# The sample tokens' RWKV matrices: groups of 32 tokens in 32-column and 32x32 tiles, in place of masked 128x128 matrices

## The chip, the cores and the metric

The kernel runs on one core of a Trainium2 chip. The metric is device microseconds of one execution, from which a median is taken; smaller is better. The engines are TensorE (PE in the profile, with its weight loads as PEld), VectorE (DVE), ScalarE (ACT), GpSimd (POOL) and SyncE (SP), whose queue issues most of the transfers. Each works through its own list of instructions in order and waits on semaphores of the others.

## The reference

One layer of a hybrid encoder is computed for two groups of tokens: one prompt of 256 tokens, and 8 samples of 16 tokens each, which continue from a cached state. The layer has an RWKV-7 branch, a sparse-attention branch, a gated mix of both, and an expert layer (PEER). The change touches only the samples' part of the RWKV branch. Its recurrence, per head with a 64x64 state S:

```python
def _rwkv7_step(S, inp):
    r, w, k, v, a, b = inp
    sa = jnp.einsum('bhij,bhj->bhi', S, a)
    S = S * w[:, :, None, :] + sa[..., None] * b[:, :, None, :] + v[..., None] * k[:, :, None, :]
    y = jnp.einsum('bhij,bhj->bhi', S, r)
    return S, y
...
    S_fin, ys = lax.scan(_rwkv7_step, S0.astype(f32), xs)
```

There are 16 heads. Tokens of different samples never meet in it: the 8 samples are 8 independent scans of 16 steps.

## The kernel before

The scans are not run step by step. For a stretch of tokens the recurrence is written with small triangular matrices: one that couples the tokens' a and b vectors (MB), one that couples a or r with k (MK), and the inverse of a unit triangular matrix (T). For the prompt the stretch is 64 tokens, for a sample its 16 tokens.

Heads are handled in pairs, eight of them, by `rwkv_pair`; a pair's 128 columns are two heads of 64. The 128 sample tokens of all 8 samples stand together on the 128 partitions. For each pair `rwkv_pair` makes, for MB and for MK and for each head, the 128x256 product of b (or k) with the two rows a and r of all 128 sample tokens, one fp32 matmul with 64 rows of contraction, 128 columns of weights and 256 moving columns, into a PSUM tile `fx` (two buffers), and VectorE multiplies it with the mask `ms` into `MBs` or `MKs`. The mask keeps the 16x16 blocks on the diagonal and zeroes the rest. Four such matmuls stand in each pair.

`rwkv_inverse` writes the a-b half of `MBs` to DRAM (`As`), reads the 16x16 blocks back with one block on a partition (`NL`), inverts 48 blocks at once on VectorE by 15 steps of forward substitution (the prompt's blocks are among them), writes the result to a DRAM matrix (`Bs`, zeroed once, two in turn), and reads that back as a 128x128 matrix per head, `TTs`.

`chain_s` uses them: W = A0 + MK v, U = T W, y = A0' + MB U + MK' v, each with 128x128 weights and 64 moving columns per head: two matmuls for W, two for U, four for y, in fp32. A0 and A0' are added by a matmul with the identity. W and U pass through VectorE copies from PSUM to SBUF, y through a ScalarE copy.

All matmuls of these helpers go through `mm` (line 226), so that most of PE's rows in the profile have that line; tile names tell them apart. `tp` is the place in the array, and operands of 64 or 32 rows or columns occupy a part of the array only.

The stage in which the pairs run also holds dense projections (`mm` tiles, weights split in a high and a low float32r half), the attention of the samples and the prompt (`dx`, `cKT`, `cV` tiles) and the modulation (`w_ada`). The string `ORDER` says in which order the pieces are issued; the framework's scheduler, which works from a simulated timeline, then places their instructions on the engines, so that pieces are interleaved and a changed instruction can move others. The tile pools set how far each can run ahead. Later stages (mix, expert scores, expert sums) are untouched by the change.

## Time and profile before

| | |
|---|---|
| median of 3 runs | 1801.76 us (1797.88 to 1802.8) |
| the profiled execution | 1796.01 us, span 1794.1 us |
| PE busy | 1714.5 us, 96% of the span, 12576 matmul records |
| DVE busy | 1362.0 us, 76% |
| ACT, POOL busy | 703.2 us, 700.5 us |
| the stage of the pairs | about 140 to 720 us of the span |

The span runs from the first to the last instruction; the profiled execution's own time is 1.9 us longer. In rows of the timeline the columns are start, duration, engine, line, operation, output<-inputs, rows*columns of the weights in the array, shape of the output and how many equal instructions were merged. The duration of a matmul includes its way through the array, which the next one overlaps: what a matmul costs PE is read from the starts of those that follow it. An fp32 matmul is recorded as two matmuls (two passes over the moving columns): `bx<-W,TTs` has 32 records for 16 matmuls.

### The profile page before, as it was taken

The page shows a single profiled execution, that of the slowest core. Times are in us where ns is not written, and L with a number is a line of the kernel's source. Part 1 is how long each engine was busy: PE and PEld are TensorE (multiplying, and loading weights), DVE is VectorE, ACT ScalarE, POOL GpSimd, SP SyncE. Part 2 cuts the span into 40 slices and gives each one's busy share as a digit, 9 for nine tenths or more (in the row PEclk, how much of TensorE's full clock was granted, in tenths as well). Part 3 has the DMA queues.
Part 4 walks back from the last instruction along what each step waited for, and adds up shares of the span by engine and source line. Part 5 has one row for each costly group of instructions (what it writes and reads, how often), then busy time and mean ns, then how long its engine had stood idle before and what let it go on. Part 6 is the DMA issues. An engine that isn't in the chain of part 4 may idle for free.

```text
span 1794.1 us, 33542 instructions
## 1 busy us (share of the span) xinstructions
PE 1714.5 (96%) x12576; PEld 1420.0 (79%) x12576; DVE 1362.0 (76%) x2945; ACT 703.2 (39%) x1411; POOL 700.5 (39%) x752
## 2 busy tenths in 40 slices
PE   6999899999999999999999989999999999999998
PEld 4987687777878877898888889999967667776656
DVE  3448777777867765445999999899958778887885
ACT  4533343333333333324222264488843333333232
POOL 2432242323423320024054446533356565555641
PEclk7999899999999999999999999999999999999999
DMA  8543652463365364665499989964579999999995
GB/s 298 161 128 96 198 178 63 155 195 97 101 198 158 85 217 151 219 202 166 151 336 333 347 305 370 376 228 164 201 267 373 364 377 379 364 395 345 376 378 182
DMA packets 181082, 434.11 MB, mean 242 GB/s; under 512 B 39348, under 2 KB 78388, under 8 KB 180920
## 3 DMA queue, kind: packets, MB, share of 16 engines
q1 hardware_dynamic: 144056, 297.73, 49.4%
q0 software_dynamic: 36864, 134.23, 20.1%
q8 instruction: 99, 1.62, 0.4%
q14 instruction: 63, 0.52, 0.1%
HBM read 401.65 MB, written 30.24 MB: 241 GB/s over the span
## 4 chain that ended last, share of the span: by engine, by line
PE 67%; DVE 15%; DMA 10%; issue 3%; ACT 2%; POOL 2%; SPq 0%; DVEq 0%; ACTq 0%; POOLq 0%
PE mm L226 24%; PE fx L226 15%; PE dx L226 12%; PE cp L226 8%; PE bx L226 7%; DVE raw L1570 2%; DMA w<-in_pv 2%; DVE wl L234 2%; DVE acc L1580 1%; DMA w<-in_w_ada 1%; DMA raw<-in_pv,pe 1%; DMA w<-in_w_in 1%; DMA w<-in_puT 1%; ACT wh L230 1%; DVE psi L1297 1%
## 5 line engine op out<-in xcount | busy, mean ns | idle before, releaser
L234 DVE TENSOR_TENSOR wl<-w,wh 128x1024 fp32r<-128x1024 f32 (+1 forms) x274 | 343.6, 1259 | 119.6 <-ACT wh L230 58.6
L230 ACT ACTIVATE wh<-w 128x1024 fp32r<-128x1024 f32 (+1 forms) x282 | 295.9, 1054 | 207.5 <-PE mm L226 83.0
L1559 POOL DMA_INDIRECT raw<-in_pu,pe x128 | 154.6, 1208 | 181.1 <-PE dx L226 56.0
L226 PE MATMUL fx<-h2h,wh 128*128 128x256 f32 x736 | 216.1, 294 | 7.5 <-ACT wh L230 4.5
L1559 POOL DMA_INDIRECT raw<-in_pv,pe x128 | 173.0, 1351 | 120.4 <-PE dx L226 44.9
L226 PE MATMUL fx<-h2h,wl 128*128 128x256 f32 x736 | 212.2, 289 | 7.7 <-DVE wl L234 7.4
L226 PE MATMUL fx<-h2l,wh 128*128 128x256 f32 x736 | 209.9, 285 | 0.0
L1580 DVE SCALAR_TENSOR_TENSOR acc<-raw,dots,acc 128x1024 f32<-128x1024 f32 x127 | 165.2, 1301 | 10.3 <-DMA raw<-in_pv,pe 9.1
L1570 DVE SCALAR_TENSOR_TENSOR raw<-raw,sh 128x1024 f32<-128x1024 f32 x128 | 161.8, 1274 | 12.5 <-DMA raw<-in_pu,pe 11.7
L226 PEld LDWEIGHTS fx<-h2h,wh 128*128 128x128 f32 x736 | 140.9, 191 | 12.3 <-ACT wh L230 5.9
L226 PEld LDWEIGHTS fx<-h2h,wl 128*128 128x128 f32 x736 | 140.2, 191 | 10.7 <-DVE wl L234 10.1
L226 PEld LDWEIGHTS fx<-h2l,wh 128*128 128x128 f32 x736 | 141.2, 192 | 2.2 <-issue 1.7
L226 PE MATMUL fx<-h2f,w 128*128 128x256 f32 x576 | 129.9, 387 | 6.0 <-ACT G L1471 3.1
L226 PEld LDWEIGHTS fx<-h2f,w 128*128 128x128 f32 x576 | 111.0, 194 | 23.2 <-ACT G L1471 4.0
L226 PE MATMUL mm<-LTh,wh 128*128 128x384 f32 (+2 forms) x352 | 125.1, 356 | 3.3 <-ACT wh L230 2.7
L226 PE MATMUL mm<-LTh,wl 128*128 128x384 f32 (+2 forms) x352 | 123.3, 350 | 0.6 <-DVE wl L234 0.6
L226 PE MATMUL mm<-LTl,wh 128*128 128x384 f32 (+2 forms) x352 | 122.8, 349 | 0.0
L226 PE MATMUL mm<-wh,LTh 128*128 128x256 f32 x336 | 97.9, 292 | 2.7 <-ACT qx L879 2.7
L226 PE MATMUL mm<-wh,LTl 128*128 128x256 f32 x336 | 97.6, 290 | 0.0
L226 PE MATMUL mm<-wl,LTh 128*128 128x256 f32 x336 | 97.3, 290 | 0.0
L1393 POOL TENSOR_TENSOR G<-G,wg 128x144 f32<-128x144 f32 (+1 forms) x64 | 55.5, 889 | 95.6 <-ACT wg L1390 95.6
L1471 ACT ACTIVATE G<-fx 128x256 f32<-128x256 f32 x76 | 28.8, 383 | 122.8 <-PE fx L226 116.6
(560 smaller groups left out, 4193.2 us busy)
## 6 DMA issues: line engine op xcount, KB each, us to landing
w<-in_puT SPq DMA_DIRECT2D x128, 512.0 KB
w<-in_pv SPq DMA_DIRECT2D x128, 512.0 KB
w<-in_w_in SPq DMA_DIRECT2D x70, 512.0 KB
w<-in_w_ada SPq DMA_DIRECT2D x48, 512.0 KB
cKT<-in_cKT SPq DMA_DIRECT2D x32, 256.0 KB
cV<-in_cV SPq DMA_DIRECT2D x32, 256.0 KB
w<-in_w_pq SPq DMA_DIRECT2D x16, 512.0 KB
d<-wst SPq DMA_DIRECT2D x8, 832.0 KB
```

Source lines behind the costliest of these rows:

```text
L226: return self.nc.tensor.matmul(out, l, r, start=start, stop=stop, skip_group_check=True, **kw)
L230: self.nc.scalar.activation(hi, src, AF.Copy)
L234: (self.nc.vector if eng == "v" else self.nc.gpsimd).tensor_tensor(lo, src, hi, op=OP.subtract)
L1297: nc.vector.max_index(si[:, half, h, 8:16], sv[:, half, h, 8:16], s2)
L1393: (nc.vector if w is p else nc.gpsimd).tensor_tensor(g, g, w[:, :, c0:c1], op=OP.mult)
L1471: nc.scalar.activation(g, p, AF.Gelu_apprx_tanh)
L1559: d = nc.gpsimd.indirect_dma_start(out=u, out_offset=None, in_=src, in_offset=bass.IndirectOffsetOnAxis(ap=e[:, j:j + 1], axis=0))
L1570: nc.vector.scalar_tensor_tensor(u, u, 1.0, h2, op0=OP.mult, op1=OP.mult, accum_out=dots[:, j:j + 1])
L1580: nc.vector.scalar_tensor_tensor(acc, v, dots[:, j:j + 1], acc, op0=OP.mult, op1=OP.add)
```

## The change

`ms` is folded to 32 columns per half: row p of the mask speaks of the 32 tokens of p's group. For MB and MK, each head's product is made in four matmuls, one for each group of 32 tokens (two samples), with 32 weight columns and 64 moving columns (32 of a, 32 of r), each into its own 32 PSUM partitions; the PSUM tile has 64 columns instead of 256, and so have `MBs`, `MKs` and VectorE's multiplications. `As` and `Bs` hold 32x32 blocks; each is written or read by one DMA for each head, two where one stood. `TTs` has 32 columns per head. In `chain_s` each matmul with `MK`, `TT` or `MB` becomes four with 32x32 weights on the array's diagonal, and for y the MK part is issued ahead of the MB part.

```diff
-    same = (p[:, None] // 16) == (p[None] // 16)
-    c["ms"] = np.concatenate([same & (p[:, None] < p[None]), same & (p[:, None] <= p[None])], 1).astype(np.float32)
+    q = p[:, None] // 32 * 32 + np.arange(32)[None]
+    same = (p[:, None] // 16) == (q // 16)
+    c["ms"] = np.concatenate([same & (p[:, None] < q), same & (p[:, None] <= q)], 1).astype(np.float32)
...
+G32 = [slice(g, g + 32) for g in range(0, 128, 32)]
...
-            b = self.dt_([64, 516])
-            nc.sync.dma_start(b, z[:64, :516])
+            b = self.dt_([66, 128])
+            nc.sync.dma_start(b, z[:66, :128])
...
-            m_s = self.t([128, 2, 256], tag=tg + "s", bufs=2)
+            m_s = self.t([128, 2, 64], tag=tg + "s", bufs=2)
...
-            p = [self.ps([128, 256], tag="fx") for _ in prs]
+            p = [self.ps([128, 64], tag="fx") for _ in prs]
             for par, pr in enumerate(prs):
-                self.mm(p[par], src[pr, 0:128], ARs[pr].rearrange("p a l -> p (a l)"), tp=(64 * par, 0))
+                for gr in G32:
+                    self.mm(p[par][gr].rearrange("p (a l) -> p a l", a=2), src[pr, gr], ARs[pr, :, gr], tp=(64 * par, gr.start))
...
-        nc.sync.dma_start(sub_ap(As, 0, [[128, 128], [16512, 2], [1, 128]]), MBs[:, :, 0:128])
+        bs = lambda t, par: sub_ap(t, 4224 * par, [[1056, 4], [32, 32], [1, 32]])
+        for par in range(2):
+            nc.sync.dma_start(bs(As, par), MBs[:, par, 0:32])
...
-        ls = lambda t: sub_ap(t, 0, [[2064, 16], [128, 16], [1, 16]])
+        ls = lambda t: sub_ap(t, 0, [[528, 16], [32, 16], [1, 16]])
...
-        TTs = self.t([128, 2, 128], tag="TTs")
-        nc.sync.dma_start(TTs, sub_ap(Bs, 0, [[128, 128], [16512, 2], [1, 128]]))
+        TTs = self.t([128, 2, 32], tag="TTs")
+        for par in range(2):
+            nc.sync.dma_start(TTs[:, par], bs(Bs, par))
...
         for h in range(2):
-            self.mm(pw[:, hs(h)], MK[:, h, 0:128], vi[:, hs(h)], start=False, stop=True)
+            for gr in G32:
+                self.mm(pw[gr, hs(h)], MK[gr, h, 0:32], vi[gr, hs(h)], start=False, stop=True, tp=(gr.start, gr.start))
...
         for h in range(2):
-            self.mm(pu[:, hs(h)], TT[:, h], W[:, hs(h)])
+            for gr in G32:
+                self.mm(pu[gr, hs(h)], TT[gr, h], W[gr, hs(h)], tp=(gr.start, gr.start))
...
         for h in range(2):
-            self.mm(py[:, hs(h)], MB[:, h, 128:256], U[:, hs(h)], start=False, stop=False)
-            self.mm(py[:, hs(h)], MK[:, h, 128:256], vi[:, hs(h)], start=False, stop=True)
+            for gr in G32:
+                self.mm(py[gr, hs(h)], MK[gr, h, 32:64], vi[gr, hs(h)], start=False, stop=False, tp=(gr.start, gr.start))
+        for h in range(2):
+            for gr in G32:
+                self.mm(py[gr, hs(h)], MB[gr, h, 32:64], U[gr, hs(h)], start=False, stop=True, tp=(gr.start, gr.start))
```

Three places of PE's list, before and after. In the names, `mm` tiles are dense projections, `A` is A0, and the number behind a tile's name is its buffer. An `x4` in these lists counts matmuls as the program has them. First the product of b with a and r for one head of the first pair, before:

```order
L226 MATMUL mm_2485<-wl_2456,LTh_168 128x256
L226 MATMUL fx_1396<-ARs_1371,kk_1339 128x256
L226 MATMUL mm_2485<-wh_2455,LTl_169 128x256
L226 MATMUL mm_2485<-wh_2455,LTh_168 128x256
L226 MATMUL mm_2485<-wl_2456,LTh_168 128x256
```

The same place after the change:

```order
L230 MATMUL mm_2561<-wh_2531,LTl_169 128x256
L230 MATMUL mm_2561<-wh_2531,LTh_168 128x256
L230 MATMUL fx_1396<-ARs_1371,kk_1339 32x64 x4
L230 MATMUL fx_1407<-ARp_1372,kk_1339 64x128 x4
L230 MATMUL mm_2561<-wl_2532,LTh_168 128x256
```

One matmul has become four, and the prompt's products (`ARp`) now follow at once. Second, W of the first pair in `chain_s`, before:

```order
L226 MATMUL mm_4365<-wh_4361,LTh_168 128x256
L226 MATMUL bx_1695<-cfirst,A_314_1674 128x128
L226 MATMUL bx_1695<-vn_1445,MKs_1413 128x64 x2
L226 MATMUL dx_2991<-kT_2444,qTp_2443 128x128 x2
L226 LDWEIGHTS idb
```

and after:

```order
L230 MATMUL bx_1709<-cfirst,A_314_1688 128x128
L230 MATMUL bx_1709<-vn_1457,MKs_1419 32x64 x6
L230 MATMUL cp_1659<-Sb_1582,NX_1609 64x64 x2
L230 MATMUL bx_1709<-vn_1457,MKs_1419 32x64 x2
L230 MATMUL dx_3067<-kT_2520,qTp_2519 128x128 x2
```

The eight matmuls with 32x32 weights are parted by two of the prompt's chain with 64x64 weights. Third, y of the first pair, before:

```order
L226 MATMUL bx_1704<-cfirst,A_314_1674 128x128
L226 MATMUL bx_1704<-U_1694,MBs_1393 128x64
L226 MATMUL bx_1704<-vn_1445,MKs_1413 128x64
L226 MATMUL bx_1704<-U_1694,MBs_1393 128x64
L226 MATMUL bx_1704<-vn_1445,MKs_1413 128x64
L226 MATMUL dx_3012<-vv_2445,set_3016 128x64 x2
```

and after:

```order
L230 MATMUL bx_1730<-cfirst,A_314_1688 128x128
L230 MATMUL bx_1730<-vn_1457,MKs_1419 32x64 x8
L230 MATMUL bx_1730<-U_1708,MBs_1393 32x64 x8
L230 MATMUL dx_3088<-vv_2521,set_3099 128x64 x2
L230 MATMUL mm_4569<-wh_4507,LTl_169 128x256
```

Four matmuls have become sixteen, with the ones with MK ahead of those with MB.

## The prediction

> **What bounds the kernel now.** I read the page first: the busy time of each engine and the chain that ended last.

> ```profile
> span 1794.1 us, 33542 instructions
> PE 1714.5 (96%) x12576; PEld 1420.0 (79%) x12576; DVE 1362.0 (76%) x2945; ACT 703.2 (39%) x1411; POOL 700.5 (39%) x752
> PE 67%; DVE 15%; DMA 10%; issue 3%; ACT 2%; POOL 2%; SPq 0%; DVEq 0%; ACTq 0%; POOLq 0%
> ```

> Two thirds of the chain are PE's. The pairs all lie in one stage, so I asked for the busy time of that stage alone, and for what PE waited for in it (us in total, times, longest).

> ```profile
> core 0: us, PE busy (x) PEld busy (x) DVE busy (x) ACT busy (x) POOL busy (x), PEclk, DMA share, GB/s
> 140.00:720.00 580.00, 563.45 (x6065) 459.78 (x6064) 427.30 (x1162) 203.94 (x495) 173.17 (x254) 0.98 0.48 147
> PE dx L948 <- DVE qr L872: 3.6, 2, 3.0
> PE mm L226 <- ACT qx L879: 2.7, 2, 1.6
> ```

> PE is idle for 580.00 − 563.45 = 16.6 us, in small pieces. DVE is busy for 427 of 580 and ACT for 204. So PE's work sets the end of this stage, and what follows it starts when it ends: a microsecond off PE here is nearly a microsecond off the end.

> **What the change touches on PE.** Per pair there are four products with `ARs` and eight matmuls in `chain_s`. Their price is what they push the dense matmuls apart. First a product with `ARs`, in the timeline of PE (a product is one matmul, two passes, x2):

> ```profile
> 159.47 0.28 PE L226 MATMUL mm<-wl,LTh 128*128 128x256 f32 x1
> 159.68 0.70 PE L226 MATMUL fx<-ARs,kk 64*128 64x256 f32 x2
> 160.31 0.39 PE L226 MATMUL mm<-wh,LTl 128*128 128x256 f32 x1
> 160.53 0.28 PE L226 MATMUL mm<-wh,LTh 128*128 128x256 f32 x1
> ```

> From the dense start ahead of it to the second one behind it are 1.06 us. Two dense steps of 0.12 would stand there anyway (the rows 272.63 and 272.75 below are such a step), so the visit costs 0.82.

> Then two visits of 64x64 tiles, with 4 and with 16 passes of 64 moving columns:

> ```profile
> 271.93 0.28 PE L226 MATMUL mm<-wh,LTl 128*128 128x256 f32 x1
> 272.14 0.33 PE L226 MATMUL cp<-Sb,NX 64*64 64x64 f32 x4
> 272.40 0.39 PE L226 MATMUL mm<-wh,LTh 128*128 128x256 f32 x1
> 272.63 0.28 PE L226 MATMUL mm<-wl,LTh 128*128 128x256 f32 x1
> 272.75 0.28 PE L226 MATMUL mm<-wh,LTl 128*128 128x256 f32 x1
> ```

> ```profile
> 243.31 0.34 PE L226 MATMUL mm<-LTl,wh 128*128 128x384 f32 x1
> 243.58 0.68 PE L226 MATMUL cp<-TN,NO 64*64 64x64 f32 x16
> 244.19 0.44 PE L226 MATMUL mm<-LTh,wl 128*128 128x384 f32 x1
> 244.47 0.34 PE L226 MATMUL mm<-LTh,wh 128*128 128x384 f32 x1
> 244.64 0.34 PE L226 MATMUL mm<-LTl,wh 128*128 128x384 f32 x1
> ```

> The first costs 0.70 − 0.24 = 0.46, the second 1.16 − 0.35 = 0.81 (the step there is 0.17 to 0.175). Twelve passes more cost 0.35: 0.029 a pass. What is left of the first, 0.46 − 4 × 0.029 = 0.34, is the price of going to another tile shape and back, 0.17 a switch. So the `ARs` product is 0.34 of switches and 0.48 of passes, 0.24 for 256 columns or 0.06 for 64.

> U of `chain_s` uses the whole array, as the dense matmuls do, and pays no switch:

> ```profile
> 530.55 0.34 PE L226 MATMUL mm<-LTh,wh 128*128 128x384 f32 x1
> 530.73 0.55 PE L226 MATMUL bx<-W,TTs 128*128 128x64 f32 x4
> 531.09 0.42 PE L226 MATMUL mm<-LTl,wh 128*128 128x384 f32 x1
> 531.34 0.34 PE L226 MATMUL mm<-LTh,wl 128*128 128x384 f32 x1
> ```

> It costs 0.79 − 0.35 = 0.44 for four passes, 0.11 each, though only 64 columns move: that is nearer to loading 128 columns of weights than to moving 64. W has the same form. The eight passes of y, from the first to what follows them:

> ```profile
> 277.80 0.33 PE L226 MATMUL bx<-U,MBs 128*128 128x64 f32 x2
> ...
> 278.64 0.61 PE L226 MATMUL dx<-vv,set 128*128 128x64 f32 x4
> ```

> 0.84. So `chain_s` has 2 × 0.44 + 0.84 = 1.72 us of such passes in a pair.

> **Part by part.** Removed on PE: 32 `ARs` products (8 pairs × 4) × 0.48 = 15.4 us of passes, and 8 × 1.72 = 13.8 us in `chain_s`: 29.1 us together.

> Added: 128 matmuls for the `ARs` products, 256 passes, and 8 × 32 = 256 matmuls in `chain_s`, 512 passes: 768 passes of 64 moving columns on tiles of 32 columns. No row has such a tile with so few columns. The two nearest prices are the two-abreast 0.029 above (two 64x64 tiles on the diagonal) and this place, where a `cp` and a `bx` group use all four 64x64 tiles:

> ```profile
> 262.20 0.22 PE L226 MATMUL cp<-MBp,cQ 64*64 64x64 f32 x1
> 262.21 0.22 PE L226 MATMUL bx<-cQ,bn 64*64 64x64 f32 x1
> 262.21 0.22 PE L226 MATMUL cp<-MBp,cQ 64*64 64x64 f32 x1
> 262.21 0.22 PE L226 MATMUL bx<-cQ,bn 64*64 64x64 f32 x1
> 262.26 0.22 PE L226 MATMUL cp<-MBp,cQ 64*64 64x64 f32 x1
> ...
> 262.27 0.22 PE L226 MATMUL cp<-MBp,cQ 64*64 64x64 f32 x1
> ```

> Four passes start within 0.01 us, the next four 0.06 us later: 0.015 a pass with four tiles at work. The new groups have four tiles each (four diagonal ones, or four column groups of one row half), so I take 0.015: 768 × 0.015 = 11.5 us. With 0.029 it would be 22.3.

> Switches: I counted in both programs' lists how often PE's tile shape changes from one matmul to the next: 556 times before, 603 after. The `ARs` products only change one partial shape for another; `chain_s`, which paid nothing, now goes to 32x32 and back 26 times, and some groups are parted, as W of the first pair is. 47 × 0.17 = 8.0 us.

> Sum on PE: 11.5 + 8.0 − 29.1 = −9.6 us; with 0.029 a pass, +1.2. Below −9.6 there is room only if both heads' products run together on eight tiles, at half the price for 256 passes: −1.9 more. The order keeps most of them apart.

> Not on the path: VectorE's 32 mask multiplications.

> ```profile
> L605 DVE TENSOR_TENSOR MBs<-fx,cfront x16: 394/421/425, 157.0 to 613.1; 128x256 f32<-128x256 f32 x16
> L672 SPq DMA_DIRECT2D d<-MBs x8: 359/374/378, 160.9 to 613.6; - x8
> SPq L672 <- DVE MBs L605: 20.3, 4, 8.2
> ```

> At 0.42 us and a quarter of the columns they can save at most 32 × 0.42 = 13 us of DVE's 427, where DVE is not the bound: nothing, covered by PE; were that cover gone, a gain and no loss. The DMAs move a quarter of the bytes in as many pieces, each a quarter as long, and one more write and one more read is issued per pair: 16 × 0.37 = 6 us of SP's queue over the stage. The write waits for MBs (20.3 us in 4 waits), with the weight loads behind it in the queue; now two writes wait, the first for one head and the second for both, so the last of them goes no later than the one before did. I price this at nothing, with the loads ahead in four buffers as cover; if that fails, the loss is of the size of the issue, 6 us at most.

> How much reaches the end: between the chain's PE share, 0.67, and all. I take 0.8, since PE's idle pieces in the stage are few: −7.7 us. The rearranged order can add to or take from the 16.6 us that PE idles; I allow 5 us either way, about a third of it.

> The sum is against the profiled execution, 1796.0 us (span 1794.1 and 1.9 around it): 1788.3. The median of the runs shown is 5.8 above it, and the same step from there gives 1794.1.

> **The rivals.** *A pass costs 0.029 however many tiles there are* (no change). Long runs of small passes in this trace keep that pace whatever they move; with 32 moving columns instead of 64 too:

> ```profile
> 696.32 1.12 PE L226 MATMUL bx<-ARs,S 64*64 64x32 f32 x32
> 697.24 0.34 PE L226 MATMUL cp<-Sb,NX 64*64 64x64 f32 x4
> ```

> That is 0.92 for 32 passes, 0.029 each. If PE cannot start passes faster for long, PE's sum is +1.2 us and the time 1803. Against it: the eight passes at 262.20, and that those 32 have 64-column weights and two tiles only. [...]

> *The diagonal tiles take turns at the PSUM bank* (slower). The four 32x32 tiles write one PSUM tile. If only one may write at a time, a pass of 64 columns costs its full 0.06: 512 × 0.06 = 30.7 us in `chain_s` instead of 13.8, with the `ARs` part at 256 × 0.015 = 3.8 instead of 15.4 and the switches at 8.0: +13.3 us on PE, +10.6 at the end, 1812. It decides for slower from (29.1 − 8.0 − 3.8) / 512 = 0.034 a pass. Against it: `cp<-TN,NO` has two diagonal tiles writing one PSUM tile, at 0.029 and not 0.06. [...]

> *The gain is swallowed* (no change). PE has less to do, and the chains through DVE, ACT and the DRAM round trip of the inverse, which the change hardly shortens, come due: the 9.6 us turn into waits such as the two quoted above. For it: the scheduler has moved many rows. Against it: 16.6 us idle in 580. The time is then about 1802.

> **How the numbers follow.** A measurement of this kernel can tell about 0.3%, 5.4 us, from no change: faster is below 1796.4, slower above 1807.2. Forecast 0.58, of which 0.42 is faster and 0.16 within; the pace of 0.029: 0.17 (0.02, 0.12, 0.03 slower); swallowed: 0.13 (0.03, 0.07, 0.03); the turns at the bank: 0.12 (0, 0.03, 0.09). Together 0.47, 0.38, 0.15. The range begins at −9.6 − 1.9 − 5 = −16.5, 1785, and ends at the 0.029 pace with 5 us of order against it, +6.2, 1808; the turns at the bank are left out above it.

> **What would show it.** Right: a visit of eight 32x32 matmuls (x16) between dense ones costs near 0.34 + 16 × 0.015 = 0.58, an `ARs` product of x8 near 0.46; in the stage PE's idle stays near 16 us, and the last pair's y comes 7 to 10 us earlier. Wrong: x16 costs 0.8 (the pace) or 1.3 (the turns), a switch costs well over 0.17 (at 0.37 the gain is gone), or the idle time grows by as much as the busy time shrinks.

## The result: 0.8% slower, and the profile after

The changed kernel takes 1817.06 us (median of 5 runs, 1813.83 to 1822.73) against 1801.76 us (5 runs): the ratio is 1.0082 [1.0055, 1.0110]. I had forecast 1794.1, with a range that ended at 1808.

```profile
span 1820.3 us, 34699 instructions
PE 1727.3 (95%) x13152; PEld 1428.2 (78%) x13152; DVE 1359.6 (75%) x2945; ACT 703.3 (39%) x1411; POOL 678.6 (37%) x752
PE 63%; DVE 17%; DMA 11%; issue 5%; ACT 2%; POOL 2%; SPq 0%; DVEq 0%; ACTq 0%; POOLq 0%
```

This profiled execution took 1822.3 us, near the slow end of its five times; that of before, 1796.0 us, lies below all five of its own. PE's share of the chain fell from 67% to 63%; DVE, DMA and issue took it over. Aligned instruction by instruction with the profile before, PE was 9.5 us **ahead** at 375 us, level at 460, and 15 us behind from 725 to 1325 us, which is the difference of the medians. (Another 10 us of this execution's distance come after 1325 us, where nothing was changed; whether the kernel's other runs have them too is not shown, since they were not profiled.) So the gain was made, and then lost with 15 us on top, all within the stage of the pairs.

First what I had priced. An `ARs` product and U of `chain_s` between dense matmuls, in the timeline of PE after:

```profile
163.89 0.39 PE L230 MATMUL mm<-wl,LTh 128*128 128x256 f32 x1
164.11 0.28 PE L230 MATMUL mm<-wh,LTl 128*128 128x256 f32 x1
164.32 0.32 PE L230 MATMUL fx<-ARs,Xk 64*32 64x64 f32 x8
164.57 0.38 PE L230 MATMUL mm<-wh,LTh 128*128 128x256 f32 x1
164.79 0.28 PE L230 MATMUL mm<-wl,LTh 128*128 128x256 f32 x1
...
463.54 0.28 PE L230 MATMUL mm<-wh,LTl 128*128 128x256 f32 x1
463.75 0.43 PE L230 MATMUL bx<-W,TTs 32*32 32x64 f32 x16
464.11 0.39 PE L230 MATMUL mm<-wh,LTh 128*128 128x256 f32 x1
464.33 0.28 PE L230 MATMUL mm<-wl,LTh 128*128 128x256 f32 x1
```

The product costs 164.79 − 164.11 − 0.24 = 0.44 us (I said 0.46), the x16 visit 464.33 − 463.54 − 0.24 = 0.55 (0.58). For these two visits the prices were right.

Then the stage as a whole, from the first `ARs` product to the first matmul of the mix stage (length, and busy time and count of PE, PEld, DVE, ACT, POOL, then the granted clock, DMA share, GB/s); before:

```profile
156.20:723.10 566.90, 550.22 (x5988) 448.68 (x5988) 413.16 (x1125) 199.61 (x480) 167.63 (x236) 0.98 0.49 150
```

and after:

```profile
156.80:735.80 579.00, 554.70 (x6556) 452.10 (x6555) 410.07 (x1124) 200.59 (x480) 155.64 (x236) 0.94 0.47 144
```

The column to read is the granted clock, 0.94 where it was 0.98: it is 1 or 0.5 in the records, so the stage has 74 us at half clock against 27. PE's busy time rose by 4.5 us although its work fell. To separate the two I count each matmul's busy time with the clock granted at that moment: **work** is PE's time as it would be at full clock, **idle** is the length less the busy time, **clock loss** is the rest. By this count, which the tables below use, the stage before is 537.4 + 16.7 + 12.8, and after 521.0 + 24.4 + 33.6. The work fell by 16.4 us, the idle time rose by 7.7 and the clock loss by 20.8.

One place shows how they hang together. Timeline of PE after, at the fourth pair:

```profile
382.93 1.07 PE L230 MATMUL bx<-ARs,S 64*64 64x32 f32 x32
387.78 0.69 PE L230 MATMUL mm<-LTh,wh 128*128 128x384 f32 x1 [3.78 <-ACT gg L437]
388.27 0.52 PE L230 MATMUL mm<-LTl,wh 128*128 128x384 f32 x1
388.59 0.52 PE L230 MATMUL mm<-LTh,wl 128*128 128x384 f32 x1
```

and the stretches around it:

```profile
361.00:381.90 20.90, 20.90 (x270) 16.64 (x270) 13.91 (x41) 7.24 (x19) 5.21 (x10) 1.00 0.53 156
381.90:388.00 6.10, 2.32 (x53) 1.62 (x49) 2.46 (x4) 2.81 (x5) 1.32 (x2) 0.80 0.86 295
388.00:408.00 20.00, 20.00 (x246) 15.92 (x247) 13.80 (x37) 5.13 (x13) 5.11 (x12) 0.89 0.49 153
408.00:423.00 15.00, 15.00 (x89) 10.67 (x86) 7.72 (x22) 4.71 (x17) 3.20 (x4) 0.55 0.21 55
423.00:470.00 47.00, 47.00 (x605) 39.60 (x604) 35.67 (x96) 14.72 (x35) 13.38 (x25) 1.00 0.35 99
```

PE idles for 3.78 us, and the dense matmuls behind it start 0.32 us apart, twice their 0.165 to 0.175. The clock record has the cut at 385.6 us, 1.6 us into this wait. My prediction had no term for either.

A second cut covers most of 408 to 423 us: 89 matmul records in 15 us, where the stretch behind it has 605 in 47. No wait led to it. PE was busy without a break from 387.8 us on, and just ahead of the cut it went through visits of small and changing shapes, with no dense matmul from 406.9 to 411.5 us:

```profile
406.10:409.50 3.40, 3.40 (x45) 2.25 (x40) 2.07 (x8) 0.96 (x3) 0.77 (x2) 1.00 0.59 161
409.50:423.10 13.60, 13.60 (x76) 9.74 (x73) 6.93 (x18) 4.27 (x15) 2.77 (x4) 0.50 0.17 42
```

So waits and clock loss are not one thing. Of the nine cuts of this profile between 140 and 740 us, three came with less than 0.7 us of idle time in the 3.4 us before them.

The largest waits of PE in 140 to 740 us after (total, times, longest):

```profile
PE cp L230 <- DVE Sb L794: 4.5, 2, 3.6
PE mm L230 <- ACT gg L437: 3.8, 1, 3.8
PE mm L230 <- DMA w<-in_w_ada: 2.7, 1, 2.7
```

`Sb` is the prompt's chain, `gg` the sigmoid of a gate projection, `w_ada` a weight load. The change touches none of them; they stand elsewhere in the order now.

### The profile page after: what moved, and what is told of

Same layout as the page of the kernel before. It is cut to its first block, busy times and chain, and to the rows that moved or that the text cites. A ratio compares the mean times of both kernels' runs of the same rounds, so it can differ in the third digit from the quotient of the medians.

```text
span 1820.3 us, 34699 instructions
## 1 busy us (share of the span) xinstructions
PE 1727.3 (95%) x13152; PEld 1428.2 (78%) x13152; DVE 1359.6 (75%) x2945; ACT 703.3 (39%) x1411; POOL 678.6 (37%) x752
## 4 chain that ended last, share of the span: by engine, by line
PE 63%; DVE 17%; DMA 11%; issue 5%; ACT 2%; POOL 2%; SPq 0%; DVEq 0%; ACTq 0%; POOLq 0%
PE mm L230 22%; PE fx L230 14%; PE dx L230 11%; PE cp L230 7%; PE bx L230 7%; DVE raw L1583 2%; DVE acc L1593 2%; DVE wl L238 2%; DMA w<-in_puT 2%; DMA raw<-in_pu,pe 2%; DMA raw<-in_pv,pe 1%; ACT wh L234 1%; DMA w<-in_w_in 1%; DMA w<-in_w_ada 1%; DVE psi L1307 1%
## 5 line engine op out<-in xcount | busy, mean ns | idle before, releaser
L1572 POOL DMA_INDIRECT raw<-in_pu,pe x128 | 150.8, 1178 | 186.5 <-PE dx L230 53.4
L1572 POOL DMA_INDIRECT raw<-in_pv,pe x128 | 168.1, 1313 | 131.5 <-PE dx L230 55.1
L230 PEld LDWEIGHTS mm<-LTh,wh 128*128 128x128 f32 (+2 forms) x352 | 68.9, 196 | 10.7 <-ACT gg L437 3.9
```

Of the source, the lines that this page charges most:

```text
L230: return self.nc.tensor.matmul(out, l, r, start=start, stop=stop, skip_group_check=True, **kw)
L1572: d = nc.gpsimd.indirect_dma_start(out=u, out_offset=None, in_=src, in_offset=bass.IndirectOffsetOnAxis(ap=e[:, j:j + 1], axis=0))
```

## The experiments

Theory A: the scheduler's new order of the other instructions lost the time. Theory B: the small tiles themselves lost it. To part them I built kernels with the instructions of every engine held in a given order: the kernel whose order is wanted is built first, and its order is put on the other as edges that order issue only and wait for nothing; a changed group stands where the old one stood. In the profiles PE's records outside the changed groups stand as in the kernel before but for at most 15 of 12128 places, where in the changed kernel 4450 differ. The edges leave nothing else in the program: `half_columns` below, which has them, has 33544 instructions where the kernel before has 33542, in the same order on TensorE, VectorE, ScalarE and GpSimd but for two records. `q` holds an engine's instructions, sorted by the wanted order:

```diff
+    for (_, _, x), (_, _, y) in zip(q, q[1:]):
+        tc.add_manual_dep(y, x.name, mybir.DependencyInfo(mybir.DependencyClass.NoSync, mybir.DependencyReason.DATA))
```

**New tiles in the old order.** 

> The changed kernel (32-column products, 32x32 tiles in chain_s, its DMAs) with the instructions of every engine held in the order of the kernel before: each changed group stands where the old one stood. Theory A, the new order of the other instructions loses the time (PE idles, the granted clock is cut): with the old order the priced gain shows, 1802 - 8 = about 1794 us, ratio 0.995 or 0.996, and the clock between 140 and 740 us stays near 0.98. Theory B, the small tiles themselves lose it (stretches of partial tiles count as little work and cut the clock): the loss stays, 1812 to 1820 us, and the clock of that stage is near 0.95, as in the changed kernel.

Measured: 1798.58 us, ratio 0.9990 [0.9973, 1.0007]. The loss is gone, so B falls. But A's gain of 8 us (0.9955) is not there either: it lies outside the interval. The stage:

```profile
155.90:718.60 562.70, 538.28 (x6564) 438.91 (x6563) 406.37 (x1125) 199.00 (x480) 165.22 (x236) 0.98 0.48 148
```

Work 525.8, 11.6 us less than before; idle 24.5, 7.8 more; clock loss 12.4, the same. The waits that grew, in the same stretch (lines of this kernel):

```profile
PE mm L290 <- ACT qx L984: 3.3, 3, 1.8
PE mm L290 <- DMA w<-in_w_ada: 3.0, 2, 1.9
PE cp L290 <- DVE NX L858: 2.3, 2, 1.6
...
PE dx L1228 <- ACT se L1224: 1.7, 2, 1.0
```

Before, they were 2.7, 1.6, 1.1 and 0.8. PE comes earlier, what it waits for does not.

**Old tiles in the new order.** 

> The kernel before (128x256 products, 128x128 tiles, one DMA each) with the instructions of every engine in the order that the changed kernel has. Theory A (order): it carries the loss without the gain, 1817 + 8 = about 1825 us, ratio 1.013, with the clock of 140 to 740 us near 0.94. Theory B (tiles): about the time before, 1802 us, within 4, and the clock there near 0.98.

Measured: 1806.75 us, 1.0056 [1.0028, 1.0084]. A's direction, less than half of its size, and B's bound of 1806 is passed by less than 1 us. Its twelve times fall in two groups, seven from 1798.9 to 1807.4 us and five from 1817.2 to 1821.7. The profiled execution (1819.9) is of the second and has in the stage

```profile
155.70:734.40 578.70, 560.00 (x5979) 455.83 (x5978) 417.20 (x1123) 200.19 (x480) 156.13 (x236) 0.95 0.48 146
```

work 534.5, idle 18.7, clock loss 25.5: with the old tiles too, this order is cut by the clock, from 410.7 and from 523.4 us, as the changed kernel is from 409.5 and 522.1. The first again has no wait in the 3.4 us ahead of it.

**Parts of the change, in the old order.** The products alone; `MBs` and `MKs` keep 256 columns, and `g4` views them as 2x4x32:

```diff
-                self.mm(p[par], src[pr, 0:128], ARs[pr].rearrange("p a l -> p (a l)"), tp=(64 * par, 0))
+                for gr in G32:
+                    self.mm(p[par][gr].rearrange("p (a l) -> p a l", a=2), src[pr, gr], ARs[pr, :, gr], tp=(64 * par, gr.start))
-                nc.vector.tensor_tensor(m_s[:, par], p[par], self.c["ms"], op=OP.mult)
+                nc.vector.tensor_tensor(g4(m_s[:, par]), p[par].rearrange("p (a l) -> p a l", a=2).unsqueeze(2).to_broadcast([128, 2, 4, 32]),
+                                        g4(self.c["ms"]), op=OP.mult)
```

> Only the products with ARs are made in groups of 32 columns; the mask multiplication spreads them into the old 128x256 layout, chain_s and the DMAs are as before, the order is that of before. Theory A: by the prices of the prediction 15.4 - 3.8 = 11.6 us less on PE, nearly all of it at the end: 1791 to 1794 us. Theory B: 32-column products of one row half are small work too, so part of the loss: 1802 to 1810.

Measured: 1803.99, 1.0017 [0.9994, 1.0040]. A missed by 10 us, though the work of the stage fell by 10.5 us (526.9): idle rose by 5.5 and clock loss by 5.6. The time lies in B's range, 1802 to 1810, so this run alone does not part the two; the run with 64x64 tiles further down, which has no narrower tile than its neighbours, came out at the same time. And `chain_s` alone, shown for W:

```diff
-            self.mm(pw[:, hs(h)], MK[:, h, 0:128], vi[:, hs(h)], start=False, stop=True)
+            for gr in G32:
+                self.mm(pw[gr, hs(h)], MK[gr, h, gr], vi[gr, hs(h)], start=False, stop=True, tp=(gr.start, gr.start))
```

> Only chain_s uses 32x32 tiles (it reads the diagonal blocks of the old 128x256 layout); products and DMAs as before, in the order of before. By the prices: 13.8 us of passes removed, 512 x 0.015 = 7.7 added, 35 more switches of shape x 0.17 = 6.0 us: nothing, 1802 within 3 (theory A). Theory B: the 32x32 groups cut the clock: 1808 to 1818.

Measured: 1803.80, 1.0017 [0.9997, 1.0037], which is A's number, though not A's way: the stage has 3.4 us less work (534.0) where A had none, and 6.4 more clock loss in the profiled execution.

**Does a busy PE on small tiles keep its clock?** A program of its own; its tiles on the diagonal are

```diff
+        def diag(n, w):
+            for k in range(n):
+                g = slice(k * w % 128, k * w % 128 + w)
+                mm(small[g, 0:64], src[g, 128 * (k % 4):128 * (k % 4) + w], src[g, 512:576], (g.start, g.start))
```

> No part of the model: PE alone, without a wait, in stretches of some 30 us between dense ones (128x384 on the whole array): 2400 passes of 32x32 tiles with 64 moving columns on the diagonal, 1200 of 64x64 tiles, 2400 of 64x32 tiles, 320 of the whole array with 64 columns, then 32x32 and 64x64 visits in turn, then one, three and six dense matmuls between visits of sixteen 32x32 passes; the outputs are zeros. Theory C (the clock follows how much of the array is at work): in the stretches of 32x32, 64x64 and 64x32 tiles and of visits in turn the granted clock falls to 0.5 though PE never waits, with six dense matmuls a visit it stays at 1.0. Theory D (only an idle PE loses the clock): 1.0 in all of them. The pace: 0.015 us a pass of 32x32 and of 64x32 over the long run if the prediction's price holds, 0.029 by its rival of the pace, 0.06 by that of the turns at the bank.

Stretches of 32x32, 64x64, 64x32 tiles (the fourth row is the rear part of the third) and of visits in turn (same columns as above):

```profile
78.30:111.80 33.50, 20.11 (x1201) 18.70 (x1200) 0.00 (x0) 0.00 (x0) 0.00 (x0) 0.92 0.02 4
154.40:172.00 17.60, 17.60 (x601) 17.54 (x600) 0.00 (x0) 0.00 (x0) 0.00 (x0) 1.00 0.02 5
213.80:246.00 32.20, 29.93 (x1201) 28.53 (x1200) 0.00 (x0) 0.00 (x0) 0.00 (x0) 0.58 0.02 5
222.10:246.00 23.90, 23.53 (x841) 22.52 (x840) 0.00 (x0) 0.00 (x0) 0.00 (x0) 0.50 0.02 5
349.00:374.00 25.00, 25.00 (x642) 18.55 (x641) 0.00 (x0) 0.00 (x0) 0.00 (x0) 1.00 0.01 3
```

and two bursts of the first:

```profile
93.94 1.99 PE L209 MATMUL small<-src 32*32 32x64 f32 x128 [1.47 <-issue]
97.40 1.99 PE L209 MATMUL small<-src 32*32 32x64 f32 x128 [1.47 <-issue]
```

Theory C falls for 64x64 tiles and for visits in turn, which kept the full clock for 17.6 and 25 us. The two stretches that lost it are those in which PE stood idle, 13.4 and 2.3 us of them, with nothing to wait for that the profile shows. That is D's way. But D does not hold either: after its two gaps of 1.1 and 0.8 us the stretch of 64x32 tiles stayed at half clock, though from 222.1 us on PE was busy for 23.5 of 23.9 us. So in this run the clock was lost where PE stood idle, and those 23.5 us busy on small tiles did not win it back. The pace is 1.99 / 128 = 0.0155 us a pass, as priced, and 3.46 / 128 = 0.027 over the long run, because after 128 passes there is a gap of 1.47 us. The visits of the kernel are far shorter than that.

**A new order with no new tile.** Two matmuls of y change places in the code, nothing else:

```diff
-            self.mm(py[:, hs(h)], MB[:, h, 128:256], U[:, hs(h)], start=False, stop=False)
-            self.mm(py[:, hs(h)], MK[:, h, 128:256], vi[:, hs(h)], start=False, stop=True)
+            self.mm(py[:, hs(h)], MK[:, h, 128:256], vi[:, hs(h)], start=False, stop=False)
+        for h in range(2):
+            self.mm(py[:, hs(h)], MB[:, h, 128:256], U[:, hs(h)], start=False, stop=True)
```

> The kernel before with one thing changed: in chain_s the two matmuls of y with MK are written ahead of the two with MB, as in the changed kernel; tiles, DMAs and sizes as before. The scheduler moves about as many instructions for it as for the whole change. Theory A (a new order by itself moves the time): off the time before by 5 us or more, most likely slower, 1807 to 1817, with PE's work as before and the difference in idle time and clock. Theory B (the tiles): 1802 within 3.

Measured: 1809.06 us, 1.0036 [1.0011, 1.0061].

```profile
156.90:731.20 574.30, 555.00 (x5980) 450.57 (x5979) 415.08 (x1124) 200.56 (x480) 168.10 (x236) 0.97 0.48 147
```

Work 536.6 (before 537.4), idle 19.3, clock loss 18.4: the same work, 7.4 us longer. Theory A, with nothing else in play; here the interval leaves 1 out.

**The new tiles in yet another order.** The changed kernel with y written head by head again, MB ahead of MK:

```diff
         for h in range(2):
             for gr in G32:
-                self.mm(py[gr, hs(h)], MK[gr, h, 32:64], vi[gr, hs(h)], start=False, stop=False, tp=(gr.start, gr.start))
-        for h in range(2):
-            for gr in G32:
-                self.mm(py[gr, hs(h)], MB[gr, h, 32:64], U[gr, hs(h)], start=False, stop=True, tp=(gr.start, gr.start))
+                self.mm(py[gr, hs(h)], MB[gr, h, 32:64], U[gr, hs(h)], start=False, stop=False, tp=(gr.start, gr.start))
+            for gr in G32:
+                self.mm(py[gr, hs(h)], MK[gr, h, 32:64], vi[gr, hs(h)], start=False, stop=True, tp=(gr.start, gr.start))
```

> The changed kernel with one thing put back: the matmuls of y are written head by head, MB ahead of MK, as in the kernel before. Same tiles, same DMAs; the scheduler moves nearly as many instructions for it as for the whole change. Theory A (each new order brings its own waits and clock cuts): anything from 1795 to 1815, not the 1817 of the changed kernel; the time less what the granted clock takes stays at 1757 within 4. Theory B (the tiles cost it): 1814 to 1820.

Measured: 1802.60 us, 0.9988 [0.9960, 1.0016]. Same tiles, same DMAs, 14 us less than the changed kernel. B is out a second time. (Less its mean clock loss of 49 us the time is 1754, near the lower edge of what I expected.) A's range for the time, 20 us wide, was no test by itself. Where the gain went in this one shows in its profile: aligned with before, PE is 15.8 us ahead at 650 us, 4.4 ahead at 700 and 1 at 750. The end of the stage, here

```profile
620.00:700.00 80.00, 75.20 (x1052) 58.25 (x1048) 44.01 (x117) 27.44 (x67) 9.08 (x10) 0.94 0.61 198
700.00:719.10 19.10, 10.25 (x50) 8.10 (x44) 6.57 (x15) 4.31 (x12) 1.84 (x2) 0.52 0.34 116
```

and before:

```profile
620.00:700.00 80.00, 78.88 (x1020) 63.82 (x1021) 49.80 (x138) 29.46 (x68) 12.49 (x10) 1.00 0.65 209
700.00:723.10 23.10, 20.96 (x150) 15.68 (x148) 12.40 (x33) 6.87 (x22) 4.17 (x4) 0.71 0.26 87
```

The last pair's matmuls of y end at 694.9 instead of 703.7, 8.8 us earlier, but the mix stage begins 4.0 us earlier only, after this wait for the last pair's output to come back through DRAM:

```profile
718.10 1.01 PE L230 MATMUL mm<-pbh,wh 128*128 128x384 f32 x2 [6.64 <-ACT pbh L234]
```

PE has run out of dense work there, and what is left of the last pair and of the attention, short steps on four engines and a way through DRAM, sets the end, with a mean clock of 0.52.

**Two more orders, with the products in one case.** Products with 32 columns, and with 64 tokens a group, ordered anew; the 64-token ones also in the old order. The edit is that of the products above, with

```diff
-                for gr in G32:
+                for gr in (slice(0, 64), slice(64, 128)):
```

> Only the products with ARs in groups of 32 columns, as in the run with the order held, but the scheduler orders it anew. Theory A: PE's work in the stage is again some 10 us less than before; the time is anything between 1790 and 1815 according to the idle time and the clock that its order brings. Theory B: the same as with the order held, 1804 within 4.

> The products in groups of 64 tokens: 64x64 tiles as their neighbours ARp have, so that the shape changes 530 times in the program and not 556; chain_s and DMAs as before, order by the scheduler. On PE 32 x (0.48 - 8 x 0.029) = 7.9 us of passes and 26 x 0.17 = 4.4 us of switches less. Theory A: work in the stage 12 us less, the time between 1788 and 1813 by its order. Theory B: 64x64 tiles do as the old ones, 1790 to 1796.

> The products with ARs in groups of 64 tokens on 64x64 tiles, in the order of before (without the new order that cost 1806.5). Theory A: 7.9 us of passes and 18 x 0.17 = 3.1 us of switches less and no new waits: 1793 to 1797, faster than before. Theory G (at the margin the stage waits for others): 1799 to 1803.

Measured: 1807.98, 1.0029 [1.0004, 1.0054]; 1806.51, 1.0021 [1.0004, 1.0039]; and in the old order 1803.89, 1.0003 [0.9980, 1.0026]. The stage of the second:

```profile
155.70:732.20 576.50, 549.24 (x6044) 453.74 (x6043) 410.72 (x1124) 198.80 (x480) 155.05 (x236) 0.95 0.48 147
```

Work 520.1, 17.3 us less than before, and all of it back as 10.6 us of idle time and 16.3 of clock loss. A's ranges for the first two were 25 us wide and hold both; B's 1790 to 1796 for the 64-token products is missed by 10, while the 32-column ones lie at the upper edge of B's 1800 to 1808. The third missed A's forecast by 7 us. Its profiled execution (1792.8 us, at the fast end of its runs) has 11.3 us less work, 6.5 more idle and 2.3 more clock loss in the stage; the median has no gain at all.

**The DMAs.** Split without new tiles (new order), and the new tiles without the split (old order; both edits of the parts above together):

```diff
-        nc.sync.dma_start(sub_ap(As, 0, [[128, 128], [16512, 2], [1, 128]]), MBs[:, :, 0:128])
+        for par in range(2):
+            nc.sync.dma_start(sub_ap(As, 16512 * par, [[128, 128], [1, 128]]), MBs[:, par, 0:128])
-        nc.sync.dma_start(TTs, sub_ap(Bs, 0, [[128, 128], [16512, 2], [1, 128]]))
+        for par in range(2):
+            nc.sync.dma_start(TTs[:, par], sub_ap(Bs, 16512 * par, [[128, 128], [1, 128]]))
```

> The kernel before with the write of As and the load of TTs issued as two DMAs each, one a head, as in the changed kernel but with the old pieces; no tile changes. It brings 16 more issues and a new order. If the two DMAs cost what I bounded (at most 6 us) and the order is innocent: 1801 to 1808. Theory A: 5 to 15 us above before by its order, 1807 to 1817, with the clock below 0.976.

> The 32-column products and the 32x32 tiles of chain_s, but with the DMAs and the 128x256 layout of before (the mask multiplication spreads the products), in the order of before. If the DMA part is free, as I priced it, the same as with it, 1798.6 within 3. If the split DMAs in small pieces cost their 16 x 0.37 = 6 us of issue: 1792 to 1795.

Measured: 1806.72, 1.0017 [0.9996, 1.0037], and 1802.16, 0.9988 [0.9965, 1.0011]. With the order held, the ratio is 0.9988 without the DMA part and 0.9990 with it: it costs nothing that can be seen, within some 4 us by the intervals. (The time itself is 0.6 us above the "1798.6 within 3", in a series whose kernel before was 1.3 us slower.) The split in a new order came out where an innocent order was expected, 1801 to 1808, and its interval holds 1. So its time says nothing for A, though its mean clock over the runs, 0.974, is below the 0.976 that A names.

**Work in the waits, to keep the clock.** Matmuls ahead of the ones that waited:

```diff
+        for _ in range(WARM.get(self.calls, 0)):
+            self.nc.tensor.matmul(self.spares[out.tensor.name], self.LT[0][:, 0, 0:128], self.LT[0][:, 1, 0:128],
+                                  start=True, stop=True, skip_group_check=True)
+        self.calls += 1
```

Other than the first expectation says, some of the sums come out wrong with them: they stand with `start=True` in PSUM tiles that other matmuls use, and that this is the way is my reading. Sizes, counts and order do not depend on these sums.

> The changed kernel in its own order, with 171 matmuls of 128x128 by 128 columns added on PE, whose results nobody reads (they go to unused columns of a PSUM tile): they stand right ahead of 13 matmuls that PE waited for in the profile of the changed kernel, so that they fill the wait, and at three places between small tiles at 406 and 468 us. Theory E (the clock cuts after PE's waits are what costs, and work put into the waits prevents them): half-clock time between the first product and the last y falls from 58 us to under 25 and the time from 1817 to 1800 to 1806. Theory F (the waits themselves cost it, the clock only goes along): 1815 to 1820, since the waits stay.

> The changed kernel held in the order of before (1798.6 us), with 145 such idle matmuls ahead of 16 places at which PE waited in that run's profile. Theory E: half-clock time of the stage from 20 us to under 8, and 1790 to 1794 us, faster than both kernels. Theory F: 1797 to 1801.

Measured: 1826.83, 1.0144 [1.0111, 1.0178], and 1805.95, 1.0027 [1.0005, 1.0049]. Both theories missed both times. E's part on the clock did better: from the first product to the last y half clock fell from 58.0 to 30.7 us (under 25 expected) and from 20.5 to 6.8 (under 8). Over all runs the mean clock loss (time × (1 − mean clock)) did fall, from 61 to 53 us and from 43 to 37, but the work of the stage rose by 21 and 16 us (541.9 and 541.7) and only 5 and 10 of these came out of the idle time. So the added work went with less clock loss, but it cost more than that brought. That the waits of one execution are not those of the next, so that work ahead of a matmul that happens not to wait is paid in full, is my reading and not shown: each kernel has one profile.

**Less and more work in the old order, with no new tile.** 128 moving columns instead of 256 (w = 128), and each product twice (n = 2):

```diff
-                self.mm(p[par], src[pr, 0:128], ARs[pr].rearrange("p a l -> p (a l)"), tp=(64 * par, 0))
+                for _ in range(n):
+                    self.mm(p[par][:, 0:w], src[pr, 0:128], ARs[pr].rearrange("p a l -> p (a l)")[:, 0:w], tp=(64 * par, 0))
```

> The kernel before in its own order, with the products with ARs made for the first 128 of their 256 moving columns only (the second half, that with r, is left out and the mask takes the first half twice): 32 x 0.24 = 7.7 us less on PE with no new tile shape, no new order, no other DMA. Theory G (at the margin this stage waits for other engines, so PE's gain turns into idle time): at most a third reaches the end, 1798.5 to 1802, with 4 us or more idle time added. Theory H (PE sets the end): 1794 to 1796.

> The kernel before in its own order, with each product with ARs made twice into the same PSUM tile: 32 x 0.48 = 15.4 us more on PE. Theory H (PE sets the end): 13 to 16 us more, 1814 to 1817. Theory G: PE's waits take up part of it, 5 to 11 us more, 1806 to 1812.

Measured: 1798.70, 0.9985 [0.9962, 1.0007], and 1816.71, 1.0078 [1.0052, 1.0104].

```profile
155.50:722.20 566.70, 548.98 (x5987) 453.78 (x5987) 414.66 (x1126) 199.94 (x480) 166.08 (x236) 0.97 0.48 150
```

```profile
157.50:744.50 587.00, 572.10 (x6052) 466.99 (x6052) 415.47 (x1125) 199.94 (x480) 168.61 (x236) 0.96 0.47 144
```

15.4 us more of work by the prices, 11.3 by the count of the stage (548.7), cost 14.9 us, as H says. 7.7 us less by the prices, 6.0 by the count (531.4), brought 3.1. That is G's number, but the interval of −6.8 to +1.3 us does not leave out H's, and it is not G's way: idle rose by 0.9 us only, and the profiled execution has 4.8 more of clock loss.

All but the two with added matmuls, with their mean clock loss over the runs of each (before: 38 to 40 in the four series):

| kernel | tiles | order | ratio | clock loss, us |
|---|---|---|---|---|
| changed | new | its own | 1.0082 | 61 |
| tiles_old_order | new | of before | 0.9990 | 43 |
| tiles_no_dma_old_order | new | of before | 0.9988 | 42 |
| after_y_as_before | new | its own | 0.9988 | 49 |
| old_tiles_new_order | old | of changed | 1.0056 | 46 |
| nudge_y | old | its own | 1.0036 | 48 |
| dma_split | old | its own | 1.0017 | 47 |
| products_old_order | products | of before | 1.0017 | 45 |
| chain_old_order | chain_s | of before | 1.0017 | 41 |
| products_free | products | its own | 1.0029 | 49 |
| products64_free | products of 64 | its own | 1.0021 | 58 |
| products64_old_order | products of 64 | of before | 1.0003 | 41 |
| half_columns | old, half | of before | 0.9985 | 41 |
| products_twice | old, twice | of before | 1.0078 | 40 |

In the order of before the clock loss is 40 to 43 us whatever is cut from the work (45 for the products alone); in every other order it is 46 to 61. The two nearest, 45 and 46, are not apart by these means.

## Why the prediction was wrong

**PE's prices: right.** 0.34 for two switches, 0.015 a pass on four tiles. The visits cost 0.44 and 0.55 where I said 0.46 and 0.58; between them eight passes more cost 0.11, 0.014 each, which leaves 0.33. The weight loads of the whole-array passes that I read at 0.11 start 0.11 us apart in the trace before (PEld at 277.69 us: two take 0.30, where one takes 0.19). Neither the pace of 0.029 nor the turns at the bank happened: the x16 visit would have cost 0.8 or 1.3.

**The sum on PE, −9.6: right, a little small.** With the order held, work fell by 11.6 us; in the changed kernel by 16.4, of which 2.9 go with its order (the old tiles have them too). Part by part the prices were off both ways: the products alone gave 10.5 where they say 11.6, `chain_s` alone 3.4 where they say nothing.

**"I take 0.8, since PE's idle pieces in the stage are few": wrong, the first failed step.** The three kernels that have the new tiles without the bad order, at 0.9990, 0.9988 and 0.9988, say some 2 us of 9.6: about 0.2, with nothing at all inside each interval. The 7.7 us that I took (0.9957) are outside all three, of the third only just. That PE is busy 97% of the stage says what more work costs (products_twice: 14.9 us for 11.3 counted), not what less work brings. In the old order PE's gain turned into waits for `w_ada`, `NX`, `qx` and `se`, and in after_y_as_before into the tail behind the last pair. My rival that the gain is swallowed was the right one for the tiles (I gave it 0.13), and what I held against it, 16.6 us idle in 580, was no argument.

**"I allow 5 us either way" for the order: wrong, the step that cost the sign.** It was three times too narrow and it was not even-handed. The same new tiles stand at 0.9990 in the order of before and at 1.0082 in the changed kernel's own, 17 us apart. With old tiles, new orders cost 3 (with 0 in its interval), 6.5 and 10 us; with new tiles the two orders that the scheduler made lie 14 us apart. Each redrawn order lost more to the clock than that of before, so the term should have leaned to the slow side. The larger part came through the granted clock, for which the sum had no term: idle +7.7, clock +20.8, work −16.4 in the profiled execution, and a mean clock loss of 61 us over the runs where the kernel before has 38 to 40.

**The DMAs at nothing, VectorE's gain at nothing: right** (0.9988 against 0.9990).

**What would show it.** The visits came out right. PE's idle time did not stay near 16 us, and the last pair's y came 12 us later, not 7 to 10 earlier; in after_y_as_before it came 8.8 earlier, and that did not help.

What stays open: what starts the clock's cuts, since some followed waits and the one at 409.5 us none, so that it is shown that the new order costs the time, and not by which property of it; whether half_columns, whose work fell by 6.0 us, brings 3 us, all of it or nothing; and why the median of products64_old_order has nothing of the 11.3 us that its work fell by. The twelve times of one kernel spread over 12 to 23 us, and one profile each does not show which of its runs it stands for. No version beats the kernel before by more than 0.3%: the best three that compute all of it are at 0.9988 to 0.9990, with intervals across 1.

## What to carry to other kernels

When a scheduler orders the program, a change that alters any duration or issue order is two changes; draw a second order, or hold the old one, before crediting or blaming the edit. Here PE, busy for 97% of its stage, priced added work (14.9 us for 11.3), not removed work (some 2 for 11.6): for the removed, name what PE will wait for next, at the end of the stage above all. Look at the granted clock beside the busy time: here stretches of small matmuls, some with waits of 0.5 to 4 us among them and one with none, were followed by 3.4 to 20.5 us at half speed in the profile after.

## What was unexpected of the hardware

In the run of PE alone a long run of small matmuls did not keep its pace: 128 passes of 32x32 tiles in 1.99 us, then 1.47 us in which the profile shows nothing to wait for, 0.027 us a pass in all. The page of that run has 57 packets of the instruction queue, 0.93 MB, 16 KB each, and in each of the stretches of 3.4 us from 92.9, 96.3 and 99.7 us, which hold one such burst each, the DMAs moved 5 GB/s, some 17 KB; that PE waited for these packets is my reading. These three stretches, with 1.4 us of idle time each, were followed by ones at full clock, the one from 103.1 us, with 2.0 us, by one at 0.51.
